# One-pass turns of the experts' tokens, transfers moved to GpSimd's queue, swapped routing products, an early first gather

## The chip, the cores and the metric

The kernel runs on one core of a Trainium2 chip. Its engines each follow their own list of instructions: PE (TensorE, matrix products), DVE (VectorE), ACT (ScalarE), POOL (GpSimd) and SP (SyncE, which here only issues transfers). The loads of the stationary operand into PE are shown apart from its products, as PEld. Transfers are issued from a queue of SP, ACT or POOL and carried out by 16 DMA engines. The metric is the device time of one execution in microseconds; lower is better.

## The reference

One layer of a decoder, 1024 tokens of width 1024, all in float32:

```python
y = hybrid_mixer(x, ...)                 # A, B, C below, joined by w_out
x = layer_norm(ALPHA * x + y, ...)
y = hierarchical_moe(x, ...)             # 32 experts, 2 per token
x = layer_norm(ALPHA * x + y, ...)
```

```python
h_a, h_b, h_c = jnp.split(x @ w_in, ...)
o_a = swa_sink_mixer(h_a, ...)    # banded attention with bias table and sinks
o_b = dilated_mixer(h_b, ...)     # three dilated groups, merged by their softmax sums
o_c = mla_mixer(h_c, ...)         # latent attention, 8 heads, dense causal
return jnp.concatenate([o_a, o_b, o_c], -1) @ w_out
```

```python
grp = jnp.argmax(x @ w_rg + b_rg, -1)             # 1 of 4 groups
top_val, top_idx = lax.top_k(e_logits, 2)         # 2 of the group's 8 experts
gate = jax.nn.softmax(top_val, -1) * p_grp
y = (silu(xb @ w_gate[e]) * (xb @ w_up[e])) @ w_down[e]   # rows xb of expert e
```

## The kernel before

**Precision.** A product in float32 is made of three in PE's one-pass 32-bit format (F32R): each operand is split into a high and a low part (ACT casts the high part, DVE subtracts to get the low one), and `mm3` (lines 386 to 388) adds high x high, high x low and low x high. A plain F32 product, such as the routing logits, runs in two passes. A transpose is a product whose stationary operand is the tile to be turned and whose moving operand is the identity `ident`.

**Order.** The class `Order` plans the whole kernel when it is built: each `Task` has a cost on PE, steps on other engines, and the buffers it takes and gives back; from these estimates it writes one fixed order for every engine. Each engine then works through its list, and waits where an operand isn't there. A transfer stands in the list of the engine that issues it, so a transfer that waits for its data holds up all that is behind it on that list.

**Stages**, with the times of the profile:

- Start (0 to 16 us): `startup` loads x (`xr_a`, `xr_b`, `xr_c`) and the first weights from SP and splits x into `xH` and `xL`. DVE also makes `nsnk` from the sinks `snk` here.
- Projections and attention (to about 600 us): weights `wr` come by SP, are split to `wh` and `wl`, and give queries, keys and values. Groups B1, B2, B0 and the heads A need bias tables `tb` (lines 493 to 497), read from a table `d_shear` in DRAM; the values of B1 and B2 go through DRAM (`vs_B` to `d_vb` to `vB`, line 658) to be gathered by stride. Outputs of A and B are stored in `d_o` (lines 1078 and 1138). Attention C works through 8 heads: SP loads keys and queries `kqs` and values `vC`, PE makes scores `SC`, ACT and DVE the softmax, PE turns the weights (`ptC`, line 1504) and makes `oC`.
- Output projection, norm and routing (600 to 723 us): `out_tasks` makes `y` per block of 128 tokens, DVE and ACT the norm, PE turns the normed rows (`xt`, line 1828), and `place_tasks` makes the logits `lps` (line 1852), from which DVE finds groups, experts and places; `lower` (line 1905) counts tokens per expert; `slot_index` writes the token lists `idx` and `tok`, `gates` the two weights.
- Experts (723 to 1040 us): per expert `moe_tasks` gathers its tokens `xg` (POOL, line 1998), turns them in eight transposes `gx` (`tokens`, line 2169), splits them into `xh` and `xl`, and makes `gu` (24 products), the hidden values `h` and `ht`, and `y` (12 products). Weights come in three chunks of 1 MB (`er`, line 2125), cast by ACT to `eh` and subtracted by DVE to `el`. `y` is scattered to DRAM.
- Sum over the two experts and second norm (1040 to 1097 us).

## Time and profile before

| | |
|---|---|
| median of three runs | 1099.7 us (1095.06 to 1100.32) |
| the profiled execution | 1099.06 us |
| its span, first to last instruction | 1097.4 us |
| mean granted TensorE clock | 0.960 |
| PE busy in the span | 1014.5 us, 92% |
| DVE, ACT, POOL busy | 757.9 (69%), 688.7 (63%), 193.7 us (18%) |

The busy time of an engine is the time in which an instruction of its list runs; what stands in brackets behind a row of a timeline is the idle time just before it and what ended that. A granted clock of 1.00 is 2.4 GHz, one of 0.50 is 1.2 GHz. The starts of successive products tell how long one takes; their printed durations overlap.

### The profile page before, as it was taken

How to read it: one execution, taken by the hardware profiler on the slowest of the kernel's cores; microseconds unless marked ns; L12 is line 12 of the kernel's file. 1: busy time of each engine (PE TensorE's matmuls, PEld its weight loads, DVE VectorE, ACT ScalarE, POOL GpSimd, SP SyncE). 2: the span in 40 equal slices, each digit the busy share in tenths (PEclk: the TensorE clock that was granted, in tenths of full speed). 3: DMA queues.
4: the chain of work that ended last, by engine and by line, in shares of the span. 5: the costliest groups of instructions: out<-in, count | busy, mean ns of one | idle time of the engine just before them, and what ended most of it. 6: DMA issues, size and time to landing. Idle time of an engine off the chain costs nothing. (4 is left out here: it accounts for less than half of the span.)

```text
span 1097.4 us, 16475 instructions
## 1 busy us (share of the span) xinstructions
PE 1014.5 (92%) x5643; PEld 843.3 (77%) x5643; DVE 757.9 (69%) x1609; ACT 688.7 (63%) x1445; POOL 193.7 (18%) x211
## 2 busy tenths in 40 slices
PE   6998999999899998989999998959999999999972
PEld 5897779887798887878889777847778777777730
DVE  5465565354436667869687557789899999999747
ACT  4343466265434557869666344538999888888764
POOL 1001100400100101003100133521334211221123
PEclk9998999999899998989999998959999999999986
DMA  7177723603402118383661583749999999999283
GB/s 260 52 285 278 268 75 121 187 21 103 118 1 92 48 59 219 109 246 83 203 168 68 193 296 135 294 149 336 374 376 389 390 379 380 375 378 356 90 318 151
DMA packets 71190, 231.04 MB, mean 211 GB/s; under 512 B 13012, under 2 KB 20628, under 8 KB 57536
## 3 DMA queue, kind: packets, MB, share of 16 engines
q1 hardware_dynamic: 55920, 192.18, 49.8%
q0 software_dynamic: 15184, 37.79, 10.0%
q8 instruction: 45, 0.74, 0.3%
q14 instruction: 41, 0.34, 0.1%
HBM read 191.82 MB, written 58.02 MB: 228 GB/s over the span
## 5 line engine op out<-in xcount | busy, mean ns | idle before, releaser
L2154 DVE TENSOR_TENSOR el<-er,eh 128x1024 fp32r<-128x1024 f32 x188 | 226.0, 1221 | 27.4 <-ACT eh L2152 27.4
L2152 ACT CAST eh<-er 128x1024 fp32r<-128x1024 f32 x188 | 193.7, 1056 | 7.8 <-DVE el L2143 4.1
L386 PE MATMUL gu<-eh,xh 128*128 128x512 f32 x256 | 104.6, 408 | 0.0
L387 PE MATMUL gu<-el,xh 128*128 128x512 f32 x256 | 104.2, 407 | 0.0
L388 PE MATMUL gu<-eh,xl 128*128 128x512 f32 x256 | 101.5, 397 | 0.0
L1481 ACT ACTIVATE PC<-PC,mnC 128x512 f32<-128x512 f32 (+3 forms) x96 | 58.5, 616 | 19.7 <-DVE mnC L1475 19.4
L1998 POOL DMA_INDIRECT xg<-d_x,tok x32 | 39.5, 1234 | 166.8 <-PE gx L2169 144.9
L387 PEld LDWEIGHTS gu<-el,xh 128*128 128x128 f32 x256 | 48.5, 190 | 20.8 <-DVE el L2154 10.7
L386 PE MATMUL psv_B<-wh,xH 128*128 128x256 f32 (+1 forms) x192 | 60.5, 315 | 3.6 <-ACT wh L374 3.6
L387 PE MATMUL psv_B<-wl,xH 128*128 128x256 f32 (+1 forms) x192 | 59.2, 309 | 0.0
L388 PE MATMUL psv_B<-wh,xL 128*128 128x256 f32 (+1 forms) x192 | 58.9, 307 | 0.0
L735 ACT ACTIVATE P_B<-P_B,negm_B 128x128 f32<-128x128 f32 (+1 forms) x96 | 42.4, 443 | 23.1 <-DVE negm_B L731 23.1
L2003 POOL DMA_INDIRECT d_y<-y,idx x32 | 40.3, 1260 | 93.0 <-ACT y L2207 83.6
L386 PEld LDWEIGHTS gu<-eh,xh 128*128 128x128 f32 x256 | 48.5, 189 | 10.2
L376 DVE TENSOR_TENSOR plC<-ptC,phC 128x512 fp32r<-128x512 f32 (+1 forms) x80 | 46.9, 630 | 12.7 <-ACT phC L374 12.2
L388 PEld LDWEIGHTS gu<-eh,xl 128*128 128x128 f32 x256 | 48.4, 189 | 9.4
L386 PE MATMUL y<-eh,hh 128*128 128x512 f32 x128 | 53.1, 415 | 0.7 <-ACT hh L374 0.7
L387 PE MATMUL y<-el,hh 128*128 128x512 f32 x128 | 50.5, 395 | 0.0
L388 PE MATMUL y<-eh,hl 128*128 128x512 f32 x128 | 50.4, 393 | 0.0
L374 ACT CAST phC<-ptC 128x512 fp32r<-128x512 f32 (+1 forms) x80 | 39.1, 549 | 14.1 <-PE ptC L1504 13.7
L2207 ACT COPY y<-y 128x512 f32<-128x512 f32 x64 | 37.6, 588 | 11.8 <-PE y L388 9.5
L376 DVE TENSOR_TENSOR wl<-wr,wh 128x512 fp32r<-128x512 f32 (+1 forms) x52 | 34.8, 698 | 14.5 <-ACT wh L374 14.1
(440 smaller groups left out, 2898.2 us busy)
## 6 DMA issues: line engine op xcount, KB each, us to landing
er<-in_w_gu SPq DMA_DIRECT2D x63, 1024.0 KB, 12.8
er<-in_w_dn SPq DMA_DIRECT2D x32, 1024.0 KB, 13.6
wr<-in_w_qk SPq DMA_DIRECT2D x36, 256.0 KB, 3.7
fy<-d_y SPq DMA_DIRECT2D x7, 1024.0 KB, 13.4
d_vb<-vs_B SPq DMA_DIRECT2D x16, 256.0 KB, 3.2
kqs<-d_k SPq DMA_DIRECT2D x16, 256.0 KB, 5.8
kqs<-d_qn SPq DMA_DIRECT2D x16, 256.0 KB, 6.1
vC<-d_v SPq DMA_DIRECT2D x8, 512.0 KB, 7.4
```

The source lines that it names most:

```text
L374: nc.scalar.copy(h, src)
L376: (low or nc.vector).tensor_tensor(l, src, h.bitcast(F32), ALU.subtract)
L386: nc.tensor.matmul(out, st[0], mv[0], start=start, stop=False, **kw)
L387: nc.tensor.matmul(out, st[0], mv[1], start=False, stop=False, **kw)
L388: nc.tensor.matmul(out, st[1], mv[0], start=False, stop=stop, **kw)
L735: nc.scalar.activation(p[:, i, :w], p[:, i, :w], AF.Exp, bias=negm()[:, b, hh:hh + 1], scale=-1.0, accum_out=l()[:, b, hh:hh + 1])
L1481: nc.scalar.activation(pt[:, c:c + w], pt[:, c:c + w], AF.Exp, bias=mn[:, 1:2], scale=-1.0, accum_out=sm["l"][:, b, n, i:i + 1])
L1998: self.nc.gpsimd.indirect_dma_start(out=xg, out_offset=None, in_=self.d_x1, in_offset=bass.IndirectOffsetOnAxis(ap=tok.bitcast(U32), axis= ...
L2003: return self.nc.gpsimd.indirect_dma_start(out=self.d_y, out_offset=bass.IndirectOffsetOnAxis(ap=idx.bitcast(U32), axis=0), in_=y, in_offs ...
L2152: nc.scalar.copy(hi[:, s], t[:, s])
L2154: nc.vector.tensor_tensor(lo[:, s], t[:, s], hi[:, s].bitcast(F32), ALU.subtract)
L2207: nc.scalar.copy(y[e][:, s], ps)
```

## The change

1. At the start ten F32 products of `ones` with itself (`warm`) stand on PE ahead of the first real product. `ident` becomes an F32R tile, with an F32 view of it for the other transposes. SP loads the halves of x's first two tiles in turn with the first weights; ACT issues the loads of the six other tiles between its casts (`xload`). `nsnk` is made after the split of x.
2. The four bias tables, the sixteen value stores and the stores of the outputs of A and B are issued by POOL, no longer by SP.
3. The routing logits have `wr` as stationary and the turned rows as moving operand. The result (40x128) is copied by ACT (`lt`) and turned back by PE to 128x40; each block's products are a task of their own. With this the planner writes another order in routing.
4. The first expert's tokens are gathered as soon as the token list is there, ahead of the counts and gates; sixteen `warm` products stand between the last count and `gx0`.
5. The eight transposes `gx` of each expert run with F32R operands and `ident1`.

On SP around the heads of attention C, before (`d_o` is the store of oA's outputs, `kqs0` keys and queries, `vC` values):

```order
L1613 DMA xr1_0_4581<-in_x 128x512
L1613 DMA xr1_1_4583<-in_x 128x512
L1078 DMA d_o_69<-oA0_4375 128x1024
L1078 DMA d_o_69<-oA1_4718 128x1024
L1419 DMA kqs0_4299<-d_k_74 64x1024
L1420 DMA kqs0_4299<-d_qn_75 64x1024
```

and after:

```order
L1626 DMA xr1_0_4593<-in_x 128x512
L1626 DMA xr1_1_4595<-in_x 128x512
L1432 DMA kqs0_4311<-d_k_75 64x1024
L1433 DMA kqs0_4311<-d_qn_76 64x1024
L1435 DMA kqs0_4311<-d_qr_77 16x1024 x2
```

The two stores are gone from SP; on POOL they stand directly ahead of `ofa0`, which reads what they store.

On PE in routing, before (`lower` with `oh20` is the running count of blocks 0 and 1, `y4_1` the second half of block 4's output projection):

```order
L388 MATMUL y4_0_7410<-woh7_0_7007,ol74_7237 128x512
L1905 LDWEIGHTS lower_7145
L1905 MATMUL lps0_7324<-oh20_7442,lower_7145 128x64
L1906 LDWEIGHTS ones16_7148
L1906 MATMUL lps0_7324<-run_7155,ones16_7148 128x64
L386 MATMUL y4_1_7456<-woh4_1_7047,oh4_7233 128x512
L387 MATMUL y4_1_7456<-wol4_1_7048,oh4_7233 128x512
```

and after:

```order
L390 MATMUL y4_1_7470<-woh6_1_7063,ol4_7246 128x512
L1932 LDWEIGHTS lower_7157
L1932 MATMUL lps0_7336<-oh20_7464,lower_7157 128x64
L1933 LDWEIGHTS ones16_7160
L1933 MATMUL lps0_7336<-run_7167,ones16_7160 128x64
L388 MATMUL y4_1_7470<-woh7_1_7065,oh74_7248 128x512
```

Nine products of `y4_1` stand now ahead of the count, three behind it.

On PE at the end of routing, before (`lps4`, `lps6` and `lps7` are the logits of the last four blocks, `xt7` the turns of block 7):

```order
L1852 MATMUL lps4_7768<-wr_4531,x1t5_7715 128x40 x8
L1828 MATMUL xt7_0_7826<-ident_62,x1_7140 128x128 x4
L1828 MATMUL xt7_1_7833<-ident_62,x1_7140 128x128 x4
L1852 MATMUL lps6_7838<-wr_4531,x1t6_7753 128x40 x8
L1852 MATMUL lps7_7865<-wr_4531,x1t7_7825 128x40 x8
```

and after (`lt4` to `lt7` are the copies by ACT that are turned back):

```order
L1865 MATMUL lps4_7792<-x1t5_7739,wr_4543 40x128 x8
L1841 MATMUL xt7_0_7848<-ident_62,x1_7152 128x128 x4
L1841 MATMUL xt7_1_7859<-ident_62,x1_7152 128x128 x4
L1876 MATMUL lps4_7792<-ident_62,lt4_7824 128x40
L1876 MATMUL lps4_7792<-ident_62,lt5_7844 128x40
L1865 MATMUL lps6_7866<-x1t6_7777,wr_4543 40x128 x8
L1876 MATMUL lps6_7866<-ident_62,lt6_7890 128x40
L1865 MATMUL lps7_7898<-x1t7_7847,wr_4543 40x128 x8
L1876 MATMUL lps7_7898<-ident_62,lt7_7919 128x40
```

The turning back follows the turns of block 7 for blocks 4 and 5, and its own products for blocks 6 and 7; on ACT the cast `eh0_1` stands between the copies `lt6` and `lt7`.

The diff, cut to its core:

```diff
@@ startup
+        warm = self.ps.tile([P, 512], F32, name="warm", tag="mm%d" % (MMB - 1))
+        for _ in range(WARM0):
+            nc.tensor.matmul(warm[:, :P], self.ones, self.ones, start=True, stop=True)
...
                     nc.sync.dma_start(raw[kt][:, s], self.a["xT"][kt, :, s])
-                    if kt == 0 and hf == 0:
-                        self.wload(-1)
-            else:
-                nc.sync.dma_start(raw[kt], self.a["xT"][kt])
+                    self.wload(-1, 1 + hf if kt == 0 else 2 + hf)
...
+                if kt < 2 or hf == 0:
+                    self.xload(raw)
...
+    def xload(self, raw):
+
+        if self.x_next < KT:
+            self.nc.scalar.dma_start(raw[self.x_next], self.a["xT"][self.x_next])
+            self.x_next += 1
@@ bias_tables, v_tasks, scale_tasks, merge_tasks
-        self.nc.sync.dma_start(tb, ap_of(self.d_shear[g], 127, [[4 * NSH - 1, P], [NSH, 4], [1, 256]]))
+        self.nc.gpsimd.dma_start(tb, ap_of(self.d_shear[g], 127, [[4 * NSH - 1, P], [NSH, 4], [1, 256]]))
...
-                    nc.sync.dma_start(self.d_o[dst], ot)
+                    nc.gpsimd.dma_start(self.d_o[dst], ot)
@@ place_tasks
+        def logits(i):
...
+            for kt in range(KT):
+                nc.tensor.matmul(ps, c_["wr"][:, kt, :], cell["x1t", b + i][:, kt, :], start=kt == 0, stop=kt == KT - 1)
+            yield
+            t = cell["lt", b + i] = self.w2.tile([40, P], F32, name="lt%d" % (b + i), tag="lt", bufs=2)
+            nc.scalar.copy(t, ps)
...
-                for kt in range(KT):
-                    nc.tensor.matmul(lps[:, 40 * i:40 * i + 40], cell["x1t", b + i][:, kt, :], wr[:, kt, :],
-                                     start=kt == 0, stop=kt == KT - 1)
+                nc.tensor.transpose(lps[:, 40 * i:40 * i + 40], cell["lt", b + i], self.ident[0:40, 0:40])
@@ moe_tasks
+        ga0 = Task(first, 0, [[("G", 0.3)]], deps=[ix, opened], alloc=["xg"])
+        ct.deps, gt.deps = ct.deps + [ga0], gt.deps + [ga0]
+        hot = Task(warm, 3.0, deps=[ga0, ct], alloc=["mm"], free=["mm"])
...
-                        nc.tensor.transpose(ps[:, i * P:(i + 1) * P], self.xg[e % XG][:, kt * P:(kt + 1) * P], self.ident)
+                        nc.tensor.transpose(ps[:, i * P:(i + 1) * P].bitcast(F32R),
+                                            self.xg[e % XG][:, kt * P:(kt + 1) * P].bitcast(F32R), self.ident1)
```

## Rows read from the trace of the kernel before

**Rows 1.** Windows: busy us (instructions) of PE, PEld, DVE, ACT, POOL; PEclk; DMA share; GB/s
```profile
455.00:480.00 25.00, 20.09 (x120) 17.93 (x121) 16.21 (x50) 17.79 (x51) 0.77 (x1) 0.86 0.79 238
...
800.00:900.00 100.00, 100.00 (x477) 79.36 (x476) 92.44 (x106) 92.39 (x131) 30.02 (x21) 1.00 1.00 384
```

**Rows 2.** Timeline of PE at the start: start, duration, instruction, [idle <-releaser]
```profile
11.44 0.79 PE L387 MATMUL ps_c<-xL,wh 128*128 128x512 f32 x1
...
15.83 0.39 PE L388 MATMUL ps_c<-xH,wl 128*128 128x512 f32 x1
...
16.06 0.39 PE L386 MATMUL ps_c<-xH,wh 128*128 128x512 f32 x1
```

**Rows 3.** Timelines of SP, DVE and ACT at the start
```profile
2.67 1.38 SPq L431 DMA_DIRECT2D xr_a<-in_xT  x3
...
7.01 0.17 DVE L887 TENSOR_SCALAR nsnk<-snk 128x4 f32<-128x4 f32 x1 [5.94 <-DMA snk<-in_sinks]
...
8.84 0.62 ACT L364 CAST xH<-xr_a 128x512 fp32r<-128x512 f32 x1 [3.90 <-DMA xr_a<-in_xT]
```

**Rows 4.** Timeline of SP, 437 to 468 us
```profile
437.72 22.82 SPq L1078 DMA_DIRECT2D d_o<-oA  x2
...
460.63 0.54 SPq L1419 DMA_DIRECT2D kqs<-d_k  x1
...
465.18 2.13 SPq L1430 DMA_DIRECT2D vC<-d_v  x4
```

**Rows 5.** Timeline of PE, attention C, 456 to 474 us
```profile
456.44 0.40 PE L388 MATMUL SC<-kqs 96*128 96x512 f32 x1
...
473.39 0.58 PE L821 MATMUL oC<-phC,vC 128*128 128x256 f32 x1 [4.21 <-DMA vC<-d_v]
```

**Rows 6.** Timeline of PE, output projection and routing, 672 to 687 us
```profile
672.63 0.21 PE L1905 MATMUL lps<-oh,lower 128*128 128x64 f16 x1 [5.05 <-DVE oh L1892]
...
681.08 3.66 PE L1852 MATMUL lps<-wr,x1t 128*128 128x40 f32 x32
...
684.68 1.88 PE L1828 MATMUL xt<-ident,x 128*128 128x128 f32 x8
```

**Rows 7.** Timeline of ACT at the end of routing
```profile
711.29 1.91 ACT L2135 CAST eh<-er 128x2048 fp32r<-128x2048 f32 x1
```

**Rows 8.** Timelines of POOL, PE and DVE at the first expert
```profile
723.89 1.12 POOL L1998 DMA_INDIRECT xg<-d_x,tok  x1 [19.89 <-DVE gq L1977]
...
728.26 1.94 PE L2169 MATMUL gx<-ident,xg 128*128 128x128 f32 x8 [5.65 <-DMA xg<-d_x,tok]
...
731.66 0.68 DVE L376 TENSOR_TENSOR xl<-gx,xh 128x512 fp32r<-128x512 f32 x1
...
736.16 0.39 PE L388 MATMUL gu<-eh,xl 128*128 128x512 f32 x1
```

**Rows 9.** Groups by line and shape: xcount | busy us, mean ns | idle before
```profile
L2169 PE MATMUL gx<-ident,xg 128*128 128x128 f32 x256 | 34.9, 282 | 6.6 <-DMA xg<-d_x,tok 6.6
...
L2169 PEld LDWEIGHTS gx<-ident,xg 128*128 128x128 f32 x256 | 31.1, 145 | 11.1 <-issue 5.7 <-PE gx L2169 1.3
...
L387 PEld LDWEIGHTS gu<-el,xh 128*128 128x128 f32 x256 | 48.5, 190 | 20.8 <-DVE el L2154 10.7
```

**Rows 10.** Timeline of PE, two experts in a row, 950 to 961 us
```profile
950.50 1.03 PE L2169 MATMUL gx<-ident,xg 128*128 128x128 f32 x8
...
951.29 0.48 PE L386 MATMUL y<-eh,hh 128*128 128x512 f32 x1
...
960.22 1.03 PE L2169 MATMUL gx<-ident,xg 128*128 128x128 f32 x8
```

**Rows 11.** Last load of weights: SP's issue, landing time of that issue, ACT's use
```profile
1008.70 0.33 SPq L2125 DMA_DIRECT2D er<-in_w_dn  x1
...
er<-in_w_dn SPq DMA_DIRECT2D x1, 1024.0 KB, 16.6
...
1032.85 2.00 ACT L2152 CAST eh<-er 128x1024 fp32r<-128x1024 f32 x2 [0.24 <-PE gu L388]
```

More of the change, by code (lines that the diff above doesn't have):

```diff
@@ L513, in weights_of, with wload @@
         return [(self.a["w_uq"][i, :, s], [s.stop - s.start], g[:, i:i + 1]) for i in range(2)]
-    def wload(self, u):
-        while self.w_next < len(self.w_list) and self.w_raw < 3 and self.w_list[self.w_next][0] <= u + 2:
+    def wload(self, u, most=3):
+        while self.w_next < len(self.w_list) and self.w_raw < most and self.w_list[self.w_next][0] <= u + 2:
             uu, c, (src, shape, gain) = self.w_list[self.w_next]
@@ L913, in phase_attention @@
         there = self.startup()
+        nsnk = self.stat.tile([P, 4], F32, name="nsnk")
+        nc.vector.tensor_scalar_mul(nsnk, snk, -1.0)
         Pt, Q, TT, V = [], [], [], []
@@ L1897, in place_tasks @@
         ob = Buf("o" if b < LPSM else "mm")
-        lt = Task(choose, 1.65 * m, [("D", w) for w in (0.1 * m, 0.1 * m, 0.1 * m, 0.08, 0.13 * m, 0.12, 0.1 * m, 0.1 * m,
+        lg = []
+        for i in range(m):
+            lg.append(Task(lambda i=i: logits(i), 1.75, [("A", 0.3)], deps=deps if i == 0 else [], alloc=[ob] if i == 0 else [],
+                           free_pe=["x1t"]))
+        lt = Task(choose, 0.12 * m, [("D", w) for w in (0.1 * m, 0.1 * m, 0.1 * m, 0.08, 0.13 * m, 0.12, 0.1 * m, 0.1 * m,
                                                         0.08, 0.3 * m, 0.1, 0.09 * m)],
-                  deps=deps, alloc=[ob], free_pe=["x1t"] * m)
+                  deps=lg)
         def place():
@@ L2103, in count, with first, warm @@
             nc.vector.tensor_copy(self.cnt, ps[:, 0:32])
+        def first():
+            self.gather(self.xg[0], self.tok[:, 0:1])
+        def warm():
+            ps = self.buf("mm", [P, 512], F32, name="warm")
+            for _ in range(WARM):
+                nc.tensor.matmul(ps[:, :P], self.ones, self.ones, start=True, stop=True)
         ix = Task(lambda: self.slot_index(c_["tab"], self.idx, self.tok), 0, [[("D", 0.35)]], deps=[R[4][-1]] + R[6])
```

36 lines of the change are left out of this document (22 added, 14 removed).

## Prediction

> **What bounds the kernel now.** Windows by stage come first [rows 1]. PE is busy nearly all the time: it is the bound almost everywhere, and in the expert stage it shares that place with the DMA engines, whose share is 1.00 [rows 1]. So two things shorten the run: time in which PE waits, and time in which it runs at half its clock (1.2 instead of 2.4 GHz). The second follows the first: behind PE's wait of 4.21 us [rows 5] the clock is low for a while. Between 455 and 480 us the mean granted clock is 0.86, so 25 x 0.14 = 3.5 us were lost to it in that window alone [rows 1]. The timelines of PE and of the queues then show who made PE wait: the start [rows 2, 3], attention C [rows 4, 5], routing [rows 6, 7], the first expert [rows 8]. The expert stage is read from the spacing of two experts and from the shapes of its transposes [rows 9, 10], and from how late its weights arrive [rows 11].
>
> **Start.** PE's products run without a gap from 11.44 us, and ten of them, up to 15.83, take 4.39 us; after that each takes 0.23 (15.83 to 16.06) [rows 2]. At full clock the ten would take 2.3, so half clock costs 2.1 us. Ten warming products now run before the first real one, from about 2 us, when their operand is ready; they fill the time in which PE waits for x anyway, so I count them at nothing (were x ready at once they would cost their own length: 20 passes, each 0.109 us at full clock [rows 6], 4.4 us at half). The second part: the second half of x's first tile is SP's fifth load, issued at 2.67, and lands at 8.84; DVE stands on nsnk until 7.01, with the low part of x's first half behind it [rows 3]. In the new order this load is third, about 0.95 us earlier (two issues of SP at 1.38 / 3 = 0.46 each), and nsnk has left DVE's path. With six large x loads now issued by ACT between its casts, less is ahead of it; a load that landed in half of the 6.2 us that it takes now would gain 3 us more. I take 2. Together **4 us**, between 1 and 5. What is late next is x itself.
>
> **Queues.** Four bias tables, sixteen value stores and four outputs go to POOL's queue. Most of SP's waits for them had loads behind them that were not yet needed. One did matter: SP stood 22.8 us in front of the store of oA's outputs (issued 437.72 to 460.54) and then issued kqs and vC, the keys and values of the next heads, at 460.63 and 465.18 [rows 4]. PE had done its last product on the old kqs at 456.44 + 0.40 = 456.84 [rows 5]; that is now the only wait in front of these loads, so they go 3.8 us earlier. PE stood 4.21 us for vC at 473.39 [rows 5]; 0.4 us of that remain. I take it that so short a wait brings no half clock behind it, so the 3.5 us [rows 1] go as well: **7.2 us** together, 3.8 if the clock falls all the same. The store's wait is now POOL's; behind it stands the load of ofa, which needs the stored rows anyway. The other tables and stores on POOL I count at nothing: the first value product of group B2 comes far behind its loads. If that cover were gone, PE would wait for them as it does for vC. A rule speaks against such moves: the Trainium skill ("DMA: Bandwidth & Descriptors", section "Issuing engines are not separate DMA queues") says that all queues end on the same 16 engines and that issuing from several saves only the sequencer's time to initiate, usually small; by it this move gives next to nothing and the sum would be 7 us less. The trace differs: the row shows a sequencer that stands 22.8 us in a wait, which is no time of initiating.
>
> **Routing.** PE stood 5.05 us for DVE's oh before the running count at 672.63 [rows 6]. Nine products of y4 (9 x 0.23 = 2.1 us) now come before it, so **2.1 us** of the wait are filled; the rest (3 us) stays, and with it any half clock behind it. The logits' products change sides. Sixteen of them took 3.5 us as 32 passes of 0.109 (681.08 to 684.57) [rows 6]; from the other side I take the same length. Right behind them eight transposes took 1.5 us (684.68 to about 686.2), at half clock [rows 6]; eight such take 0.79 at full clock [rows 10]. If the swapped products leave the clock at 2.4 GHz, up to 0.8 us of that and as much of the products behind it are saved; I take 1.5. Against it: the result must be copied by ACT and turned back by PE; xt's transposes cover that once per pair, but for the last block the copy stands behind ACT's cast of 1.91 us [rows 7]. DVE has norm work to do meanwhile, so the tail costs 1.1 us, at most 3. Sum 2.1 + 1.5 - 1.1, **2.5 us**, from -1 to 5 (all of the half clock gone, nothing lost in the tail).
>
> **First expert.** The first gather starts at 723.89, after the gates [rows 8]; it now needs only the token list, about 0.8 us earlier. 16 warming products stand on PE just before that. At half clock their 32 passes take 32 x 0.218 = 7 us and end near 729.5, a bit after gx0's present start, 728.26 [rows 8], so gx0's end gains nothing; but gx1, as long as gx0's 1.94, and eight gate products, at half clock until 736.16 [rows 8], run at full: 1.94 - 1.03 [rows 10] = 0.9 us, and 8 x 0.2 = 1.6 us. DVE's xl at 731.66 [rows 8] is not moved, so no more is possible. Sum, rounded down, **2.4 us**, from 0 to 3.
>
> **Expert transposes.** Eight gx transposes take 0.79 us per expert (950.50 to 951.29), 0.099 each, and two experts are 9.72 apart [rows 10]. No row shows this operation in the new format, so it is bounded. From below: one pass where the plain format makes two, so half of what they take now, 0.05 each, 0.40 per expert. From above for the likely cases: a load of 128 columns into PE. The loads of these transposes take 145 ns, those of a 128-column product in the new format 190 [rows 9]. I take the lower end since the present loads are the short kind and I expect them to stay so with the same transpose flag. That saves 0.39 in a loop that runs through gx, the casts and the next products: 31 x 0.37 = 11.5 us by PE alone. But the DMA engines are full [rows 1]. The last weights were issued at 1008.70, landed 16.6 us later, at 1025.3, and were used at 1032.85 [rows 11]: 7.5 us in hand, and a faster PE cannot use more. **7 us**, from -2 to 8.
>
> **The sum.** 4 + 7.2 + 2.5 + 2.4 + 7 = 23.1 us. The profiled execution took 1099.06 us (span 1097.4 and 1.66 around it): 1099.06 - 23.1 = 1076.0. The median of the runs shown is 0.6 above it, so **1076.5 us**.
>
> **Rivals.** (A) The transposes gain nothing, since weight loads of 190 ns instead of 145 take the place of the second pass [rows 9]: 0.109 each, like the passes of the logits with a load of 128 columns each [rows 6], +0.08 per expert, +2.5 us in place of -7. For it: the load that such a product shows in the same format. Against it: the load may keep the transposes' length. 1076.5 + 9.5 = 1086.0. By the Trainium skill ("TensorE: Matmul & The Clock Gate", section "LDWEIGHTS (loading the stationary operand)") a load takes its columns / 1.2 ns, 107 ns for 128, and this rival would be the rule; the row of 0.099 between two transposes [rows 10] is already slightly under it, so the trace does not bear it out in full.
> (B) The queue move doesn't do what it says: kqs or vC come as late as before, held by something the profile doesn't show as the later of two waits. 1076.5 + 7.2 = 1083.7. For it: a wait is put down to what came last. Against it: the buffers are read last at 456.84 [rows 5].
> (C) Both, and the warming products give nothing at the start and at the first expert: 1076.5 + 9.5 + 7.2 + 4.5 = 1097.7, no change.
> (D) Slower: the new format runs a transpose in two passes like a full product, 0.109 x 2 = 0.218 each [rows 6]. Then gx takes 1.74 per expert, +0.95, and PE, not the DMA, sets the period: 31 x 0.95 = 29.5 us in place of -7: 1076.5 + 36.5 = 1113. The other parts give 16 us, so it decides from 0.099 + 16 / (31 x 8) = 0.16 us per transpose. Against it: other products in this format need a single pass.
>
> **How the numbers follow.** Forecast 0.50, A 0.25, B 0.12, C 0.07, D 0.06. The range must hold forecast, A and B with their unknown sizes. Low end: all upper bounds, 5 + 7.2 + 5 + 3 + 8 = 28, with some 4 us for a DMA stage that starts earlier: 1067. High end: A with the clock not kept up in attention C (+3.5) and the tail of routing at its 3 us: 1091. Outside lie C, D and little else. About 0.5% (5.5 us) is what a measurement of this kernel can tell from no change; faster by more than that holds forecast, A and B, less a little: 0.86; within 0.08; slower 0.06.
>
> **What would show it.** In the new trace: products at full clock from the first one, without a gap from about 9 us; SP's kqs right after PE's last product on it and no wait for vC with half clock behind it; gx groups of about 0.4 us and a period near 9.3 us until the weights' landing comes within 1 us of their use. It is wrong if loads of gx show 190 ns and its spacing 0.109, if POOL's queue makes PE wait for a table or vB, or if PE stands longer for DVE at the end of routing.

## The result, and the profile of the changed kernel

The changed kernel takes 1088.47 us (median of six runs, 1087.72 to 1090.98) where the kernel before takes 1099.84 on the same chip: 0.9914 of it, 95% interval 0.9900 to 0.9927. Two later comparisons on other chips gave 0.9919 (0.9891 to 0.9946) and 0.9923 (0.9906 to 0.9940). It is faster by 0.8 to 0.9%, 9 us; the difference of the first two medians is 11.4. Forecast were 23 us and 1076.5. The time lies inside the range (1067 to 1091), but less than half of the forecast gain came.

Where it went is read by laying PE's timeline before beside the one after: the same product, and how much earlier it now starts. The table gives that lead in us, at the product that stands at the named time in the kernel before; it holds three traces of the changed kernel and those of the experiments told below (the measuring run b_forms, which starts with a sequence of its own, is left out). A step between two columns is what the stage gained or lost.

| trace | 132 | 149 | 326 | 447 | 521 | 602 | 722 | 798 | 1030 |
|---|---|---|---|---|---|---|---|---|---|
| changed kernel, first | 1.7 | -3.1 | -2.1 | -1.9 | 4.1 | 4.1 | 3.7 | 6.7 | 9.8 |
| second (c_after) | -0.2 | -2.0 | -0.5 | -0.3 | 5.6 | 5.6 | 4.2 | 7.2 | 10.2 |
| third (d_after) | -0.2 | -4.0 | -5.0 | -4.9 | 1.0 | 1.0 | 1.6 | 4.5 | 7.6 |
| a1_tb_sp | 3.0 | 3.4 | 5.5 | 5.5 | 11.5 | 11.5 | 10.6 | 13.6 | 16.6 |
| a2_gx_f32 | 2.8 | -0.7 | -3.1 | -3.1 | 2.8 | 2.8 | 1.4 | 3.6 | 3.7 |
| a3_no_warm0 | 0.3 | -3.2 | -3.3 | -3.3 | 2.6 | 2.6 | 2.9 | 5.8 | 8.9 |
| a4_before_do | 0.1 | -1.6 | -1.2 | -1.1 | 4.8 | 4.7 | 5.1 | 6.5 | 6.6 |
| b_fill0 | 2.2 | -1.4 | -0.4 | -0.3 | 5.6 | 5.6 | 4.3 | 7.2 | 10.3 |
| b_norm0 | 2.2 | -1.8 | -2.0 | -1.9 | 4.1 | 4.1 | 3.9 | 5.4 | 8.5 |
| b_fillroute | 0.7 | -2.8 | -3.2 | -3.1 | 2.8 | 2.8 | 4.3 | 7.3 | 10.3 |
| c_xorder | 1.1 | -1.4 | -1.4 | -1.2 | 4.8 | 4.7 | 3.6 | 6.6 | 9.7 |
| c_warm_x0 | -0.8 | -5.3 | -5.9 | -5.9 | 0.0 | 0.0 | 0.1 | 1.0 | 4.0 |
| c_best | 2.3 | 1.5 | 1.7 | 1.9 | 7.8 | 7.8 | 9.3 | 12.2 | 15.3 |
| d_noswap | 2.2 | -1.2 | 1.6 | 1.8 | 7.7 | 7.7 | 12.3 | 15.3 | 18.3 |
| e_noswap2 | -0.9 | -5.7 | -6.8 | -6.6 | -0.6 | -0.6 | 0.0 | 2.9 | 6.0 |
| e_best_noswap | 1.9 | -0.2 | 0.1 | 0.2 | 6.1 | 6.1 | 9.9 | 11.3 | 14.4 |
| e_best2 | 2.1 | 2.7 | 5.7 | 5.9 | 11.9 | 11.9 | 14.9 | 17.8 | 20.9 |

Attention C (447 to 521) repeats within 0.1 to 0.2 us in every trace, and so do the experts (798 to 1030) in every trace with the new transposes. The first expert (722 to 798) gains 2.9 to 3.0 us in the changed kernel and in most variants, but 1.5 in b_norm0 and 1.4 in e_best_noswap, where about eight gate products behind it run at half clock again. Up to 326 us the traces differ by several us. All leads are taken against a single trace of the kernel before, and that has its own chances: a4_before_do, which is the kernel before but for one store, loses 1.7 us at the first table and gains 1.4 at the first expert, where nothing was changed in it. The stages of the first trace, in order:

Start, PE's timeline (start, duration, instruction, [idle <-releaser]):
```profile
6.25 0.78 PE L388 MATMUL ps_c<-xH,wh 128*128 128x512 f32 x1
...
7.25 0.40 PE L390 MATMUL ps_c<-xH,wl 128*128 128x512 f32 x1
...
9.38 0.49 PE L388 MATMUL ps_c<-xH,wh 128*128 128x512 f32 x1 [1.73 <-ACT xH L366]
```
Three products run on the first half of x's tile 0, then PE waits for tile 1; the fourth product starts at 9.38, 10.55 in the kernel before, where the gapless run begins at 11.44 [rows 2].

The first bias table: POOL's issue, DVE's first use, PE behind it:
```profile
135.20 0.80 POOL L508 DMA_DIRECT2D tb<-d_shear  x1 [4.67 <-DMA d_shear<-d_row]
```
```profile
140.56 0.29 DVE L744 CUSTOM_DVE_ANT_0 P_B<-S_B,tb 128x128 f32<-128x128 f32 x1 [6.19 <-DMA tb<-d_shear]
```
```profile
141.26 0.59 PE L388 MATMUL S_B<-h_kB,h_qB 64*128 64x128 f32 x2 [3.08 <-DVE negm_B L744]
```
This wait is new. Before, SP issued the table at 134.96, DVE used it at 138.69 after 2.31 us of waiting, and PE did not stop:
```profile
134.96 0.39 SPq L495 DMA_DIRECT2D tb<-d_shear  x1
```
```profile
138.69 0.29 DVE L731 CUSTOM_DVE_ANT_0 P_B<-S_B,tb 128x128 f32<-128x128 f32 x1 [2.31 <-DMA tb<-d_shear]
```
Here the lead falls from 1.7 to -3.1 us.

Attention C, the window that stands in [rows 1], and SP's loads (compare [rows 4]):
```profile
455.00:480.00 25.00, 23.31 (x167) 20.57 (x166) 21.18 (x63) 20.89 (x59) 1.32 (x2) 1.00 0.80 276
```
```profile
458.69 0.45 SPq L1432 DMA_DIRECT2D kqs<-d_k  x1
...
464.03 2.23 SPq L1443 DMA_DIRECT2D vC<-d_v  x4
```
The clock is 1.00 in place of 0.86 and PE's wait of 4.21 us [rows 5] is gone. At the product that stands at 480 us in the kernel before, the lead has grown by 7.8 us; just behind it PE, now early, stands for ACT and DVE, where it did not stop before, and 1.6 us come off again:
```profile
475.98 0.39 PE L834 MATMUL oC<-phC,vC 128*128 128x256 f32 x1 [0.90 <-ACT phC L376]
```
What stays is 6.0 us.

Routing, PE's timeline:
```profile
669.63 0.21 PE L1932 MATMUL lps<-oh,lower 128*128 128x64 f16 x1 [3.54 <-DVE oh L1915]
...
675.18 3.69 PE L1865 MATMUL lps<-x1t,wr 128*40 128x128 f32 x32
...
678.80 1.09 PE L1841 MATMUL xt<-ident,x 128*128 128x128 f32 x8
...
688.74 0.19 PE L1932 MATMUL lps<-oh,lower 128*128 128x64 f16 x1 [2.19 <-DVE oh L1915]
```
The first wait fell from 5.05 [rows 6] to 3.54 us. The swapped products take 3.69 us where the old ones took 3.66 [rows 6], and the transposes behind them 1.09 in place of 1.88 [rows 6], so the clock stayed up. But a second wait is now 2.19 us, 0.51 in the kernel before:
```profile
694.04 0.19 PE L1905 MATMUL lps<-oh,lower 128*128 128x64 f16 x1 [0.51 <-DVE oh L1892]
```
Behind it, 690.0 to 693.4 runs at half clock. The stage's sum is -0.4. Both waits repeat in all nine traces with this order (3.5 and 2.2 us); the half clock behind the second stands in three of them only. In the second trace of the changed kernel the products behind the same wait run at full clock, 0.23 us apart:
```profile
689.85 0.19 PE L1932 MATMUL lps<-oh,lower 128*128 128x64 f16 x1 [2.19 <-DVE oh L1915]
...
690.86 0.39 PE L388 MATMUL y<-woh,oh 128*128 128x512 f32 x1
691.09 0.40 PE L389 MATMUL y<-wol,oh 128*128 128x512 f32 x1
```

First expert, POOL and PE (compare [rows 8]):
```profile
720.20 1.26 POOL L2025 DMA_INDIRECT xg<-d_x,tok  x1 [20.17 <-DVE tok L1981]
```
```profile
718.76 6.33 PE L2138 MATMUL warm<-ones 128*128 128x128 f32 x32
724.89 0.86 PE L2208 MATMUL gx<-ident,xg 128*128 128x128 f32 x8
726.32 0.85 PE L2208 MATMUL gx<-ident,xg 128*128 128x128 f32 x8 [0.57 <-DMA xg<-d_x,tok]
```
The transposes take 0.86 in place of 1.94 us; the lead grows by 3.0.

Experts (compare [rows 9, 10]), PE's timeline and its weight loads between 800 and 1000 us (xcount | busy us, mean ns | idle before):
```profile
951.66 0.80 PE L2208 MATMUL gx<-ident,xg 128*128 128x128 f32 x8
...
961.21 0.80 PE L2208 MATMUL gx<-ident,xg 128*128 128x128 f32 x8
```
```profile
L2208 PEld LDWEIGHTS gx<-ident,xg 128*128 128x128 f32 x168 | 16.6, 140 | 2.9
```
The period is 9.55 in place of 9.72 us, the group before the next product 0.63 in place of 0.79: 0.079 us a transpose. Over the stage 3.1 us. It is not gained everywhere: in eight periods in a row, from about 770 to 850 us, both kernels need 9.52 us, and the lead doesn't grow. The groups are shorter there too (0.64 us, 0.79 before), but the products with x's high half take 4.04 us per expert in place of 3.86. From 780 to 830 us ACT is busy 97 to 98% of the time (88% from 850 to 870 in the kernel before) with the DMA engines' share at 1.01, as it is from 850 to 870 too; whether ACT or the transfers hold PE there is not shown.

### The profile page after: what moved, and what is told of

It reads as the page before. It is cut to its first block, busy times and chain, and to the rows that moved or that the text cites. A ratio compares the mean times of both kernels' runs of the same rounds, so it can differ in the third digit from the quotient of the medians.

```text
span 1086.7 us, 16593 instructions
## 1 busy us (share of the span) xinstructions
PE 1014.6 (93%) x5703; PEld 841.5 (77%) x5703; DVE 759.6 (70%) x1610; ACT 689.7 (63%) x1453; POOL 212.5 (20%) x235
## 5 line engine op out<-in xcount | busy, mean ns | idle before, releaser
L2025 POOL DMA_INDIRECT xg<-d_x,tok x32 | 43.7, 1367 | 159.4 <-PE gx L2208 138.0
L378 DVE TENSOR_TENSOR xl<-gx,xh 128x512 fp32r<-128x512 f32 x64 | 43.5, 684 | 0.0
```

The lines of the kernel that those rows point to most:

```text
L378: (low or nc.vector).tensor_tensor(l, src, h.bitcast(F32), ALU.subtract)
L2025: self.nc.gpsimd.indirect_dma_start(out=xg, out_offset=None, in_=self.d_x1, in_offset=bass.IndirectOffsetOnAxis(ap=tok.bitcast(U32), axis= ...
```

## Experiments

### The bias tables' queue

```diff
-        self.nc.gpsimd.dma_start(tb, ap_of(self.d_shear[g], ...))
+        self.nc.sync.dma_start(tb, ap_of(self.d_shear[g], ...))
```


> The changed kernel with one line put back: the four bias tables are loaded by SP's queue instead of POOL's. Theory (POOL's queue is late with the table): in the changed kernel DVE's first bias of group B waits 6.19 us for its table where 2.31 us stood before, and PE loses 5.0 us at 141 to 143 us (1.7 us ahead of the kernel before at 141, 3.3 us behind at 143). On SP the loss goes, at least the 3.9 us of the longer wait and at most the 5.0 us: 1088.5 - 4 to 5 = about 1084, and the wait for the table is near 2.3 us again. Rival (POOL's queue is not the cause; the table's source is ready later, or the transfer itself is slower because of the new x loads): the loss stays at 141 to 143 us and the time is 1088.5 within 1 us.

Measured: 1086.47 us, 0.9918 of the kernel before (0.9891 to 0.9945), so by the runs no difference from the changed kernel that they can tell. The trace (1081.97 us) shows the loss of the table gone, SP's issue and DVE's use:
```profile
131.60 0.38 SPq L508 DMA_DIRECT2D tb<-d_shear  x1
```
```profile
135.25 0.29 DVE L744 CUSTOM_DVE_ANT_0 P_B<-S_B,tb 128x128 f32<-128x128 f32 x1 [1.91 <-DMA tb<-d_shear]
```
From issue to use 3.65 us; in the six traces with the table on SP 3.65 to 3.95, in the thirteen with it on POOL 4.76 to 5.96 (5.36 above). The step from 132 to 149 us is +0.4 here, and over all traces with the changed start but b_forms it is -3.6 in the mean with POOL (12 traces, -1.8 to -4.8) and -0.5 with SP (4 traces, +0.6 to -2.1). So the queue costs about 3 us there: 1.5 in landing, the rest in the wait and the half clock that follow. That is shown by traces; the medians of this one kernel alone don't show it, and its trace is the fastest of its six runs. Two kernels further below differ in the table's queue and the order of x's halves alone: e_best_noswap has 0.9861 (0.9830 to 0.9892), e_noswap2 on the same chip 0.9929 (0.9902 to 0.9956), and the order of x by itself gave 1 to 2 us (c_xorder below: 0.9902, the changed kernel 0.9919). With SP, too, PE can stop for the table: three of the six traces have a wait, of 0.35 to 1.66 us. Part of the spread is another cause: ACT's copy of the bias rows waits up to 1.7 us for a store on SP's queue (q_1h into d_qn), with either queue for the table.

### The format of the experts' transposes

```diff
-  nc.tensor.transpose(ps[...].bitcast(F32R), self.xg[e % XG][...].bitcast(F32R), self.ident1)
+  nc.tensor.transpose(ps[...], self.xg[e % XG][...], self.ident)
```


> The changed kernel with one line put back: the experts' tokens are turned by F32 transposes as before, everything else as changed. Theory (the one-pass transpose is worth .099 - .079 = .02 us each, 0.155 per expert, and nothing more is lost in the weights' DMA): gx groups of 0.79 us again, the late period 9.72 instead of 9.55, and 1088.5 + 3.3 = 1091.8. Rival 1 (the transposes gain nothing, the experts' 3.3 us come from another edit such as the freer queues): 1088.5 within 1 us. Rival 2 (the forecast's 0.05 each was right for the path and the spacing in the trace misleads): 1088.5 + 7 = 1095.5.

Measured: 1092.86 us, 0.9969 (0.9947 to 0.9991). The lead no longer grows between 798 and 1030 us (3.6 to 3.7), and the period is that of before:
```profile
956.55 1.04 PE L2208 MATMUL gx<-ident,xg 128*128 128x128 f32 x8
...
966.27 1.03 PE L2208 MATMUL gx<-ident,xg 128*128 128x128 f32 x8
```
```profile
L2208 PEld LDWEIGHTS gx<-ident,xg 128*128 128x128 f32 x168 | 19.6, 140 | 2.8
```
So the format alone gives the experts' 3.0 us, and by this trace 0.8 more at the first expert (2.2 gained there, 3.0 with it). The loads' mean is 140 ns in either format.

What sets 0.079 us was measured by itself, ahead of the first product:
```diff
+  for _ in range(40): nc.tensor.matmul(warm[:, :P], self.ones, self.ones, ...)
+  for _ in range(16): nc.tensor.transpose(warm[:, :P].bitcast(F32R), z, z)              # a
+  for _ in range(16): nc.tensor.transpose(warm[:, :P], self.ident, self.ident)           # b
+  for _ in range(16): nc.tensor.transpose(warm[:64, :P].bitcast(F32R), z[:, :64], z)     # c
+  for _ in range(16): nc.tensor.matmul(warm[:, :P], z, z, ...)                           # d
+  for _ in range(16): nc.tensor.matmul(warm[:64, :P], z[:, :64], z, ...)                 # e
```


> The changed kernel with a measuring sequence ahead of its first product: 40 F32 products to raise the clock, then 16 each, back to back, of the transpose of 128 rows by 128 columns in the one-pass format (a), in F32 (b), the one-pass transpose with only 64 columns loaded (c), the plain one-pass product of 128 by 128 (d), and that with 64 columns loaded (e). Nothing of it is used; it adds some 10 us to the time. The experts' transposes take 0.079 us each in the one-pass format and 0.099 in F32, where 0.05 was forecast. Theory (the load of 128 columns sets the pace): c and e are clearly shorter than a and d, 0.05 or less. Rival 1 (a fixed distance between two products, whatever is loaded or moved): a, c, d and e all at about 0.08. Rival 2 (the pace of the experts' transposes is that of their data, being written by a DMA or read by ACT and DVE from the same bank meanwhile): a takes 0.05 here, where nothing else runs.

PE's timeline; the granted clock is 1.00 throughout:
```profile
6.39 9.58 PE L432 MATMUL warm<-ones 128*128 128x128 f32 x80
15.73 1.56 PE L434 MATMUL warm<-ident 128*128 128x128 f32 x16
17.12 1.94 PE L436 MATMUL warm<-ident 128*128 128x128 f32 x16
18.82 1.20 PE L438 MATMUL warm<-ident 128*64 128x128 f32 x16
19.86 1.95 PE L440 MATMUL warm<-ident 128*128 128x128 f32 x16
21.64 1.12 PE L442 MATMUL warm<-ident 128*64 128x128 f32 x16
22.61 0.44 PE L388 MATMUL ps_c<-xH,wh 128*128 128x512 f32 x1
```
From start to start and by 16: a 0.087, b 0.106, c 0.065, d 0.111, e 0.061 us. Half the columns loaded, and with them half the rows written, take 0.022 off the transpose and 0.050 off the plain product. The columns are in the pace, as the theory has it, though c and e don't reach 0.05, and loading and writing are not told apart; a fixed distance is refuted, and so is the data's supply, since a is slower here than among the experts. The counts say more: 40 F32 products leave 80 records, 16 F32 transposes 16. By its records an F32 transpose has one pass already. The Trainium skill ("TensorE: Matmul & The Clock Gate", section "Back-to-back issue gap") gives about 81 ns for a sustained stream of loads and products of N = 128; the 0.079 here agrees, the plain product's 0.111 does not. Its section "LDWEIGHTS (loading the stationary operand)" gives 107 ns for 128 columns; the transposes, 0.079 and 0.087 apart, lie under it, the plain product, 0.111, close to it.

### The store in front of attention C

In the kernel before, one line:
```diff
-                    nc.sync.dma_start(self.d_o[dst], ot)
+                    nc.gpsimd.dma_start(self.d_o[dst], ot)
```


> The kernel before with one line of the change: the stores of the first two output groups (oA) go to POOL's queue, all else stays. Theory (SP's 22.8 us stand in front of that store held kqs and vC back, and nothing else of the change bears on attention C): kqs is issued right after PE's last product on the old one, PE's wait of 4.21 us for vC and the half clock behind it go: 1099.7 - 6 to 7 = about 1093. Rival (the move alone gives nothing, because a second wait holds the loads, and the 6.1 us found at 468 to 486 us come of other edits, for instance the value stores on POOL): 1099.7 within 1 us. Between: 3 to 4 us, if the loads come early but the clock falls all the same.

Measured: 1090.30 us, 0.9938 (0.9920 to 0.9956) of the kernel before, 6.9 us by the medians. SP's load, PE, and the window:
```profile
458.01 0.45 SPq L1419 DMA_DIRECT2D kqs<-d_k  x1
```
```profile
470.16 0.28 PE L821 MATMUL oC<-phC,vC 128*128 128x256 f32 x1
```
```profile
455.00:480.00 25.00, 23.42 (x167) 20.87 (x168) 21.19 (x62) 21.58 (x61) 1.32 (x2) 1.00 0.85 278
```
Attention C gains 5.9 us here, with the table, the value stores and everything else as before. The theory stands: one line is worth more than half of the whole change. Of the Trainium skill's sentence ("DMA: Bandwidth & Descriptors", section "Issuing engines are not separate DMA queues") that a second issuing engine only saves the time of initiating, these rows say that it leaves out what stands behind a waiting issue; the table above shows that the queue can also matter for the transfer itself, 1.5 us from issue to use.

### The start

> The changed kernel without the ten warming products ahead of the first x product (they compute nothing that is used). Theory (they put the first product off from 4.99 to 6.25 us, and the clock that they win from 9.4 us on is lost again from 10.68 to 14.09): the three products of x's first half start at 5.0 but PE waits for the second half of x until 9.4 all the same; without the warming the clock is half from 9.4 until about 14, as long as before or a bit longer: between 1088.5 and 1088.5 + 1.5. Rival (the warming is what the start has gained): slower by 1.7 us or more, 1090.2 and above. Rival 2 (the warming only delays): faster by 1.3 us, 1087.2.

```diff
-WARM0 = 10
+WARM0 = 0
```
Measured: 1086.95 us, 0.9916 (0.9889 to 0.9942), the changed kernel's ratio:
```profile
5.94 0.79 PE L388 MATMUL ps_c<-xH,wh 128*128 128x512 f32 x1 [5.94 <-ACT wh L376]
...
11.05 0.79 PE L388 MATMUL ps_c<-xH,wh 128*128 128x512 f32 x1 [3.46 <-ACT xH L366]
```
The ten warming products are worth nothing that the runs can tell.

> The changed kernel with eight more products that compute nothing used, put behind the three products of x's first half, where PE stands 1.73 us (7.65 to 9.38) for the second half. Theory (the clock falls behind that wait, from 10.68 to 14.09 us, and costs half of 3.4 us = 1.7): with the wait filled the products from 9.4 us on run at full clock without a break; 1.0 to 1.7 us faster at 15 us, of which the later waits (1.7 us for a weight at 288 to 295, the table at 141) may give some back, so 1086.5 to 1088 where the changed kernel has about 1088. Rival (the clock falls all the same, or the filling runs past the landing of x and puts the products off): no gain at 15 us or a loss of up to 1 us.

```diff
+                    if first and not u and hf == 0 and kt == 0:
+                        for _ in range(8):
+                            self.nc.tensor.matmul(self.warm[:, :P], self.ones, self.ones, start=True, stop=True)
```
What PE waits for is the first half of tile 1, not, as the text above says, x's second half. Measured: 1088.46 us, 0.9915 (0.9881 to 0.9950), no difference. The clock is 1.00 from 8 to 30 us in this trace, but 0.50 from 34 to 36, and the lead falls from 2.6 us (at 34) to 1.0 (at 38); 1.2 us of that come back by 100 us. Other traces have that drop too (third trace of the changed kernel: 0.87 and 0.64 from 34 to 40), others not.

> The changed kernel with x's first four half tiles loaded and cast in the order in which PE uses them (first half of tile 0, first half of tile 1, then the second halves); the second halves stood between. Theory (PE's wait behind its first three products is for tile 1, which stands behind a load and a cast that PE doesn't need yet): the fourth product starts at 7.5 to 8.5 us in place of 9.4 to 11.7 (six traces of the changed kernel and its variants), 1 to 3 us earlier, and 0 to 2 us of it reach the end, since the waits at 141 and 290 us take up a part. Rival (the DMA engines set it: they move 256 KB in 0.7 us at their best and the tiles come one behind the other anyway): PE waits just as long for the second halves, no gain.

```diff
-        for kt in range(KT): ... for hf in range(2): load, split
+        for kt, hf in ((0, 0), (1, 0), (0, 1), (1, 1)): load, split
```
Measured: 1087.94 us, 0.9902 (0.9883 to 0.9922); the changed kernel beside it 1088.69. The fourth product:
```profile
9.45 0.50 PE L388 MATMUL ps_c<-xH,wh 128*128 128x512 f32 x1 [1.57 <-ACT xH L366]
```
In four traces with this order it starts at 8.93 to 9.82 us, 9.4 in the mean, in eleven others with the warming products at 9.38 to 11.70, 10.5 in the mean. It is a gain of 1.1 us and not the 7.5 to 8.5 expected as its start. What holds the landing is not shown: the DMA engines' share is 1.03 from 8 to 14 us, but 0.79 from 5 to 8, just before the tile lands. Over ten traces with the changed start as it is, the lead at 132 us is 1.1 in the mean, -0.9 to 3.0.

### Routing: who holds DVE

> The changed kernel with the second half of every block's normalization (x times a gain plus a bias) on DVE; as changed, four of the eight blocks have it on ACT and POOL. The planner then orders the routing anew. In the changed kernel PE stands 3.54 us and 2.19 us for DVE's oh, and in those stretches DVE's small steps that should take 0.17 to 0.35 us take 1.26 to 2.96 us, always while POOL works on x. Theory (POOL's work on x holds DVE up, and so made the wait that ate the routing's gain): the small steps are 0.35 us or shorter throughout, the two waits shrink by 4 us or more, and although DVE now has about 1.4 us more per block the whole is 1 to 4 us faster, 1084 to 1087 where the changed kernel has about 1088. Rival (the steps are slow for another reason, for instance because they wait for PE's logits): the waits stay within 1 us and the time is the same or, with DVE's added work, up to 3 us slower.

```diff
-NORM = '20222000'
+NORM = '00000000'
```
Measured: 1088.58 us, 0.9911 (0.9876 to 0.9945): no change in time. The rows of DVE and POOL in the changed kernel
```profile
661.06 2.66 DVE L1890 CAST f<-gi 128x2 f32<-128x2 uint32 x1
663.83 0.36 DVE L1893 TENSOR_SCALAR f<-iota,f 128x4 f32<-128x4 f32 x2
664.23 2.96 DVE L1896 TENSOR_TENSOR em<-gl,f 128x64 f32<-128x64 f32 x1
```
```profile
661.15 2.54 POOL L1827 TENSOR_TENSOR x<-x,gb 128x512 f32<-128x512 f32 x2
...
664.57 2.52 POOL L1827 TENSOR_TENSOR x<-x,gb 128x512 f32<-128x512 f32 x2
```
and of DVE without POOL's work:
```profile
661.48 0.15 DVE L1890 CAST f<-gi 128x2 f32<-128x2 uint32 x1
...
662.21 0.35 DVE L1893 TENSOR_SCALAR f<-iota,f 128x4 f32<-128x4 f32 x2
...
663.13 0.21 DVE L1896 TENSOR_TENSOR em<-gl,f 128x64 f32<-128x64 f32 x1
```
A cast of 128x2 that takes 0.15 us takes 2.66 when POOL is adding on x, and ends with POOL's work (663.72 against 663.69); em likewise (667.19 against 667.09). The Trainium skill ("SBUF — State Buffer", section "SBUF: two separate sides") states the rule: POOL and certain DVE operations share one pair of ports as an exclusive lock, and the loser blocks. The rows agree, with some 2.5 us as the price. The waits for oh fall from 8.1 us to 1.3 in all. So the first half of the theory holds and the second doesn't: around 694 us PE is 5 to 7 us further than in the changed kernel, but with all of the output projection's products used up. What is left has nothing beside it: the next 32 logits passes take 6.58 us instead of 3.69, at half clock, PE waits 5.1 us for DVE's en, and at 722 us the lead is what it was.

> The changed kernel with 16 and 10 products that compute nothing used, ahead of the running count where PE stands 3.54 us and 2.19 us for DVE's oh. The waits stay as long, PE only doesn't idle in them. Theory (the wait costs the clock behind it, half clock at 690 to 693.4 us, 1.7 us): the clock stays full through routing, and the time is 1.5 to 2 us less than the changed kernel's (about 1088). Rival (the filling runs past the arrival of oh, or the clock had other reasons): from no change to 2 us slower. Since the waits themselves stay, neither gives more than 2 us.

```diff
+            for _ in range({0: 16, 2: 10}.get(b, 0)):
+                nc.tensor.matmul(lps[:, 256:256 + P], self.ones, self.ones, start=True, stop=True)
```
Measured: 1086.41 us, 0.9885 (0.9835 to 0.9934). The products fill the waits to the end:
```profile
667.32 3.73 PE L1933 MATMUL lps<-ones 128*128 128x128 f32 x32
671.03 0.19 PE L1934 MATMUL lps<-oh,lower 128*128 128x64 f16 x1
```
The clock is 1.00 from 655 to 705 us (0.98, 0.93 and 0.89 in the changed kernel's three windows), and the stage gains 1.5 us where the changed kernel and its variants with the same routing lose 0.6 in the mean (nine traces, -1.4 to +0.6). Not all of these 2 us are the clock behind the two waits. From 655 to 700 us, where the waits stand, the lead grows by 1.6 us here (1.65 in the two traces of the best version below, which has the same filling) and by 0.1 in the mean of the nine (-0.9 to 0.6): 1.5 us are that clock. The rest is lost earlier: five of the nine lose 1.6 us near 635 us, where the clock falls behind two short waits ahead of any filling (0.66 from 630 to 635 us in the second trace of the changed kernel).

### Routing: the swap

> The changed kernel with the routing products as before: tokens loaded, the router's 40 columns moved through, no copy and no turning back. The planner orders the routing anew. Theory A (the swap keeps PE's clock up behind the logits and saves the 1.5 us that the forecast gave it, while the waits for oh cost it again): without it the eight transposes behind a logits group take 1.9 us instead of 1.0, and routing from 596 us to the token list is 1 to 3 us longer, 1089.5 to 1091.5 in all where the changed kernel has 1088.5. Theory B (the swap gives nothing, the routing is bound by DVE's steps and by the order): within 1 us of the changed kernel. Theory C (the copy and the turning back cost more than the clock gives): 1 to 2 us faster than the changed kernel.

> The changed kernel once more, on the same chip as the kernel with the old routing products, to be compared with. 0.991 of the kernel before. A third trace of it: the first x tiles land anywhere between 9.4 and 11.7 us, the token list stands near 719 us after the waits at 141 and 290 us.

> The changed kernel with the logits products the old way round, a second time. Theory (the swap costs what it gives, and the order around it is what differs): from 602 us to the running count's last product at 719 to 722 us again 3 to 5 us shorter than in the kernel before, where the changed kernel and its variants show -1.4 to +0.6, and by the median 3 to 5 us faster than the changed kernel, 1084 to 1086. Rival (the first trace was a lucky one, in its clock above all: 0.972 granted, the other runs 0.963 to 0.967): 0 to 1 us in routing, and the median that of the changed kernel, 0.992 to 0.993 of the kernel before.

```diff
-  nc.tensor.matmul(ps, c_["wr"][:, kt, :], cell["x1t", b + i][:, kt, :], ...)   # and lt, turned back
+  nc.tensor.matmul(lps[:, 40 * i:40 * i + 40], cell["x1t", b + i][:, kt, :], wr[:, kt, :], ...)
```
Measured: 0.9932 (0.9917 to 0.9947) and, a second time, 0.9929 (0.9902 to 0.9956); the changed kernel on the first of the two chips 0.9923 (0.9906 to 0.9940). In the first trace the stage gained 4.6 us, in the second 0.6, with the same order of instructions. PE at the first running count, first and second trace:
```profile
663.10 0.19 PE L1918 MATMUL lps<-oh,lower 128*128 128x64 f16 x1 [1.25 <-DVE oh L1905]
```
```profile
672.66 0.21 PE L1918 MATMUL lps<-oh,lower 128*128 128x64 f16 x1 [4.10 <-DVE oh L1905]
```
The difference is which of DVE's steps meets POOL's addition: in the second f (2.33 us) and em (2.94), in the first the cast ef (1.85). A third trace with the old products, e_best_noswap below, gains 3.9 us in the stage. That the swap keeps the clock up shows in the eight transposes behind a pair of blocks' logits: 1.09 or 1.10 us in all nine such groups of the changed kernel's three traces, but 1.59 to 1.91 us in six of the fifteen groups of the five traces with the old products. By the runs the swap as a whole is worth about 1 us, 0.0008 of the time, with intervals of twice that; by these traces the old products are ahead. Whether it gains anything stays open: what POOL and DVE make of the wait varies by more from one execution to the next.

### The warming products at the first expert

> The changed kernel itself once more, on the chip of the three kernels beside it, as what they are compared with, and for a second trace of it. Theory (the ledger of the first trace is typical): 0.991 of the kernel before, again 1 to 2 us gained by 30 us, then 4 to 5 us lost at 141 to 143 us. Rival (where the first x tiles land differs from execution to execution, and later waits take up what the start gives): the start's shift lies anywhere between +2 and -1 us, the shift at 300 us near -2 us either way.

> The changed kernel without the 16 warming products ahead of the first expert's transposes; the early gather stays. Theory (the 2.8 us gained at the first expert come of the clock alone, since the first gather starts 1.04 us after the token list, as before): the gx transposes and the first gate products run at half clock again, and the 2.8 us are lost: about 1091 where the changed kernel has about 1088.3. Rival (the gather or the new form of the transposes gave it): no loss, within 1 us.

```diff
-WARM = 16
+WARM = 0
```
Measured: 1091.76 us, 0.9938 (0.9915 to 0.9961), the changed kernel on the same chip 1088.69, 0.9919.
```profile
728.40 1.23 PE L2208 MATMUL gx<-ident,xg 128*128 128x128 f32 x8 [5.90 <-DMA xg<-d_x,tok]
...
730.85 0.76 PE L388 MATMUL gu<-eh,xh 128*128 128x512 f32 x1
```
Transposes and products are at half clock again, and the stage gains 0.9 instead of 3.0 us: 2.1 are the warming, by these two traces. The theory stands in the main (0.8 is the format, as told above). How much the warming is worth hangs on when the clock would have risen without it: here at 736.7 us, in the kernel before at 736.16, but in a4_before_do, which has no warming either, already at 727.9. The early gather is not early: in the changed kernel it begins 1.04 us after the token list (719.16 and 720.20), as it did before (1.03), so it gains what the list gains.

### The best version

> The changed kernel with three edits together: tables of biases on SP's queue, x's first half tiles in the order of use, and 16 and 10 idle products ahead of the running counts of blocks 0 and 2. If they add up: 4 to 5 us at 141 us, 0 to 2 at the start, 2 in routing; the first two share the wait at 290 us, so 5 to 7 us in all, 1081 to 1083 where the changed kernel has about 1088. Rival (the table's loss is taken up by the same later waits, as the medians of that run alone suggest, 1.3 us where its trace shows 6.9): 3 us, about 1085.

> The changed kernel with the bias tables on SP's queue, x's first half tiles in the order of use, and the logits products the old way round, without idle products in routing. If the swap costs what the trace without it showed: 3 to 5 us in routing besides the 3 us of the tables, 1081 to 1083. If it costs nothing: 3 us only, 1085 to 1086, and the version with the swap and the filled waits (e_best2) is 2 us faster.

> The three edits together (tables of biases on SP's queue, x's first half tiles in the order of use, idle products ahead of the running counts of blocks 0 and 2), a second time, for its size against the changed kernel and the kernel before: 0.985 to 0.987 of the kernel before.

Three edits on the changed kernel, all shown above: tables on SP, x's halves in the order of use, the filled waits of routing. Measured: 1083.25 us, 0.9863 (0.9841 to 0.9886) of the kernel before, with the changed kernel at 1088.69 on the same chip; and again 1082.01, 0.9863 (0.9838 to 0.9888). That beats both kernels, by 5 us the changed one. They add up nearly as hoped. With the swap undone and nothing filled (e_best_noswap) it is 1083.48, 0.9861 (0.9830 to 0.9892): the same. The window in routing of the second run of the best:
```profile
670.00:690.00 20.00, 19.98 (x117) 16.75 (x116) 15.72 (x51) 8.54 (x19) 13.23 (x16) 1.00 0.70 279
```

## Why the prediction was wrong, step by step

**The sum.** The mean steps are: start 1.1, first table -3.6, the waits to 326 us 0, attention C 5.9, routing -0.6, first expert 3.0, experts 3.0, end 0.4, together 9.2 us against the 9 measured. Forecast were 4, 7.2 for queues, 2.5, 2.4 and 7. The time lies in the range next to rival A's 1086, but not by rival A's way, since the transposes did gain.

**Start, 4 forecast, 1.1 found: mis-sized.** The step took x's second half tile for what PE waits on; it is the first half of tile 1, behind that half and a weight in ACT's order. Put ahead of them it came only 1.1 us sooner, and what holds it is not shown. The 2.1 us for the clock came in no lasting way: without the warming the ratio is the same.

**Queues, 7.2 forecast, 2.3 found: the failed step is the sentence that counts the other tables and stores at nothing.** The mechanism at attention C was right and its 7.2 us do come (7.8 at 480 us, 7.4 with the one line alone), but 1.6 are lost again at once, since PE then stands for ACT's phC, a wait that the term did not count: 5.9 stay. But the cover named for the rest was that of the value loads. The first table has no cover: it is read as soon as its chain of two stores through memory has ended. On POOL's queue it lands 1.5 us later from its issue, PE stops, the clock falls: 3.1 of the 3.6 us. The sentence behind it, that PE would wait if that cover were gone, named the risk without pricing it.

**Routing, 2.5 forecast, -0.6 found.** Filling (2.1) shortened the first wait by 1.5 us against the trace of the kernel before (5.05 to 3.54), by 0.2 against a4_before_do, which has the old order and 3.73; and the clock after the logits stayed up as forecast. The step that failed is a silent one, that PE meets no other bound in this stage. Before the second wait PE is 6.9 us ahead of the kernel before, DVE's choice, whose steps POOL holds there in either kernel, only 5.3 (oh done at 693.99 before, 688.69 now). So a wait that stood at 0.51 us grew by 1.7, in all nine traces. The 3.4 us at half clock behind it, which cost the first trace the same again, stand in three of the nine; five others lose as much near 635 us, ahead of both waits. The tail cost nothing (PE waits 0.48 and 0.40 for lt, where 1.1 were feared).

**First expert, 2.4 forecast, 3.0 found: right against this trace,** with 2.1 for the clock, as worked out from gx1 and the gate products, and 0.8 for the format, which that term left out. Its size is partly luck: the trace from which it was worked out kept half clock until 736.16 us, and a4_before_do, with the same code there, gains 1.4 of the 3.0 without the change.

**Experts, 7 forecast, 3.0 found: the failed step is the lower bound, half of 0.79 for one pass in place of two.** The rows already said otherwise: 8 records for 8 F32 transposes [rows 10], 32 for 16 products [rows 6]. What the new format saves is 0.02 of 0.099 us each. The load stayed the short kind, as expected, and rival A's mechanism, a pace set by the 128 columns, was right in kind as far as b_forms tells, with another size, 0.079 in place of 0.109. Nor does PE alone set the period, as the term took it up to the cap: in eight of the thirty periods 9.52 us is the floor of both kernels, and there the saving of 0.15 us per expert is not seen. The cap by the last weights was never reached, but nearly: the last weights, issued at 999.29, landed 21.6 us later, at 1020.9, and the cast at 1023.08 needs them.

Of the rivals, B fell: kqs came at once. C fell with it, and D fell.

## What to carry to other kernels

Ask of each transfer that is moved to another queue who waits for it, one by one: the store that blocked loads was worth 5.9 us, the table that looked alike cost 3. Count the records of an instruction before pricing a format: one record per transpose means that no second pass is there to save. And where a gain is a wait that is filled, look what the same engines do at the next wait, and repeat the trace, of the kernel before too, before a stage of 2 us is believed.

## What the runs showed of the hardware that was not expected

- A DVE step of 0.15 to 0.35 us that meets POOL's additions of 128x512 lasts until one ends: 2.66 and 2.96 us above, 2.33 and 2.90 in the kernel before.
- A table of 512 KB issued by POOL is usable 4.8 to 6.0 us later, by SP 3.65 to 3.95; the issue itself takes 0.80 us of POOL and 0.39 of SP.
- A transpose of 128 by 128 in one-pass format comes every 0.079 to 0.087 us, in F32 every 0.099 to 0.106, a plain one-pass product with 128 columns loaded every 0.111.
- The three traces of the changed kernel differ by 4.5 us in the lead at 326 us, out of where the first tiles land (the fourth product starts at 9.4 to 10.9 us), a clock drop near 35 us that some have, and the waits at 141 and 290 us.
